# Doubling steps of a block inversion on 32x32 diagonal blocks held side by side, in a two-block model on one core

## The chip, the core and the metric

The kernel runs on one core of a Trainium2 chip. The metric is device time in microseconds (us) of one execution, the median of several runs. Engines are named as in the profile: PE is TensorE's matmul stream and PEld its weight loads, DVE is VectorE, ACT is ScalarE, POOL is GpSimd.

## The reference

The reference is a two-block model on 512 tokens of width 1024 (the first block has 256 context tokens more). The first block holds a bidirectional RWKV-7 mixer, an mLSTM mixer and two convolutional feed-forward parts; the second block runs twice a hybrid mixer whose main branch is a bidirectional gated delta rule. Both recurrent mixers are linear scans with a rank-one correction. The delta rule in chunks of 64 tokens reads:

```
lmat  = where(strict, einsum(k_beta, k) * decay, 0)
sol   = triangular_solve(eye + lmat, rhs, lower=True, unit_diagonal=True)
value, k_cum = sol[..., :dv], sol[..., dv:]
def step(state, inp):                 # over the chunks
    v_new = val_n - k_cum_n @ state
    o_n   = q_dec_n @ state + attn_n @ v_new
    state = state * decay_n + k_dec_n.T @ v_new
```

RWKV-7 is a plain scan in the reference; the kernel gives it the same chunked form. So for every chunk of 64, head and direction a unit triangular 64x64 matrix has to be inverted.

## The kernel before, in words

All large projections are fp32-accurate products made of three single-pass matmuls on split operands (`mmacc`, lines 344, 347 and 348: 128x128 weights, 512 or 256 columns). They make one long stream on TensorE. The recurrent work runs beside it as background generators, called strands: each yields after a small group of instructions with a planned cost and a planned delay, and `Kern.tick` steps those that are due between two groups of the stream. Two strands that share a `mate` are held so that they step together. The order in which each engine executes its instructions is fixed when the kernel is built.

There are four RWKV strands, one for each pair of heads. Pairs 0 and 1 start while the projections still run. When the projections are over, `K.finish` steps all four strands without a stream, together with the loads and matmuls of `ada_steps` (line 558). The first part of the output projection then runs beside pairs 2 and 3, and `K.drain` ends them. A pair makes 6 inversions, each of 8 matrices: 4 matrices side by side, for two heads one above the other (64 + 64 partitions), so a page is 128 partitions by 256 columns. In each of the two hybrid layers there are two strands with two heads each; a head makes one inversion of 16 matrices on a page of 128x512.

`Chunk.inverse` doubles the size of the inverted diagonal blocks: with W the inverse (transposed) for blocks of size s, one doubling is W := W - X·(L_s·W), where L_s is the matrix masked to the off-diagonal s-blocks (line 731, POOL) and X the transpose of W within blocks of 32 (line 742, DVE). It runs for s = 2, 4, 8, 16 and 32, and each doubling has two products of 64x64 matrices: line 739, whose result ACT copies to the page Z (line 743), and line 748, whose result DVE subtracts from W (line 749). Before the first doubling W is set up for s = 2 by elementwise operations (line 1153 for the RWKV pairs, lines in `gdn_head` for the delta rule). A matmul addresses the tile of the 128x128 array that lies at its operands' partitions: the products of the upper 64 and of the lower 64 partitions are on two different 64x64 tiles.

Of the kernel before, what the change touches and what calls it, by code (L numbers as in the profile page):

```python
# [10 lines left out]
AF = mybir.ActivationFunctionType  # L11
# [3 lines left out]
ADD, SUB, MUL, MAX = ALU.add, ALU.subtract, ALU.mult, ALU.max  # L15

P = 128
# [11 lines left out]
C64 = 64  # L29
# [3 lines left out]
GKH = 1  # L33
HOLD = 1500
INV = 1.25
NQ = 5
NR = 8

# [617 lines left out]
class Chunk:  # L656


    def __init__(self, K):
        nc = K.nc  # L660
        self.K = K

        def sel(ap, pattern, base, cm):
            nc.gpsimd.affine_select(out=ap, in_=ap, compare_op=ALU.is_ge, fill=0.0, base=base,
                                    pattern=pattern, channel_multiplier=cm)


        pm = [K.const([P, 2, 2, C64], name="pm") for _ in range(2)]
        nc.gpsimd.memset(pm[0], 1.0)
        for h in range(2):  # L670
            r = slice(64 * h, 64 * h + 64)
            for d in range(2):
                for x in range(2):
                    sel(pm[0][r, d, x], [[1 - 2 * d, C64]], -x, 2 * d - 1)
        nc.vector.tensor_copy(pm[1], pm[0])
        self.pm = pm

        self.zm = {}
        for s in (1, 2, 4, 8, 16, 32):
            m = K.const([P, 2, C64], name=f"zm{s}")  # L680
# [10 lines left out]
            self.zm[s] = m  # L691
# [12 lines left out]


        self.big = K.const([P, 2, C64], name="big64")
        nc.gpsimd.memset(self.big, 0.0)
        for h in range(2):
            r = slice(64 * h, 64 * h + 64)
            for d in range(2):  # L710
                nc.gpsimd.affine_select(out=self.big[r, d], in_=self.big[r, d], compare_op=ALU.is_ge, fill=1e30,
                                        base=0, pattern=[[1 - 2 * d, C64]], channel_multiplier=2 * d - 1)

    def pads(self, page):

        return [page(name="pad") for _ in range(2)]

    def inverse(self, Wp, Lp, Xp, pads):


        K = self.K
        nc = K.nc
        n = Wp.shape[1]
        nu, nb = n // C64, n // C64 // 2
        T4, U8 = "p (d c j) -> p d c j", "p (u j) -> p u j"
        Zp, Lm = [t[:, :n] for t in pads]
        W, X, Z, L = [t.rearrange(U8, u=nu) for t in (Wp, Xp, Zp, Lm)]
        hs = [slice(0, 64), slice(64, 128)]

        def masked(s):  # L730
            nc.gpsimd.tensor_tensor(Lm.rearrange(T4, d=2, c=nb), Lp.rearrange(T4, d=2, c=nb),  # L731
                                    self.zm[s][:, ::-1].unsqueeze(2).to_broadcast([P, 2, nb, C64]), MUL)

        masked(2)
        for s in (2, 4, 8, 16, 32):
            ps = K.ps()[:, :n]
            for u in range(nu):
                for r in hs:
                    nc.tensor.matmul(ps[r, u * 64:u * 64 + 64], L[r, u], W[r, u], start=True, stop=True)  # L739
            if s < 32:  # L740
                masked(2 * s)
            nc.vector.transpose(Xp, Wp)
            nc.scalar.activation(Zp, ps, AF.Copy)  # L743
            yield INV * n, 1000
            ps = K.ps()[:, :n]
            for u in range(nu):
                for r in hs:
                    nc.tensor.matmul(ps[r, u * 64:u * 64 + 64], X[r, u], Z[r, u], start=True, stop=True)  # L748
            nc.vector.tensor_tensor(Wp, Wp, ps, SUB)  # L749
            yield INV * n, 1000  # L750


def conv3(K, dst, ps, n, w0, w1, w2):
# [261 lines left out]
def rwkv_prep(K, CH, p, loc, rkv, lo, up, bon, seen, out, pads, SV, NV):  # L1015


    nc = K.nc
    T4 = "p (d c j) -> p d c j"
    n = C64 * NB  # L1020
    U = 2 * NB
    hs = [slice(0, 64), slice(64, 128)]
    two = len(K.env.ps) > 1
    s = loc[0][0]
# [29 lines left out]
    r, kk = kq[:, :2 * n], kq[:, 2 * n:4 * n]  # L1054
# [6 lines left out]
    for d in range(2):  # L1061
        t = cs[:, dsl(d)]
        t = t if d == 0 else t[:, ::-1]
# [52 lines left out]
    for t, m in ((kk, skew(0, S + 1, C64)), (r, skew(1, S - 1, C64))):  # L1116
        t = t.rearrange(T4, d=2, c=NB)
# [10 lines left out]
    Wp = K.p1(name="W")  # L1128
# [12 lines left out]
    for hh in ((0, 1),) if two else ((0,), (1,)):  # L1141
# [5 lines left out]
                                    MUL)  # L1147
        yield 500 * len(hh), 900
    W = Wp[:, :2 * n].rearrange("p (u j) -> p u j", u=U)
    KS = []  # L1150
    for h in range(2):
        t = RK[h].rearrange(u4, u=U, x=2)[:, :, 1]
        nc.vector.tensor_tensor(W[hs[h]], t[hs[h]], CH.i64[hs[h]].unsqueeze(1).to_broadcast([C64, U, C64]), ADD)
        nc.gpsimd.tensor_copy(t[hs[h]], KQ5[hs[h], 1])
        KS.append(t)
    ps = K.ps()
# [4 lines left out]
    Lp, Xp = b, kd  # L1161
    Lc = K.p1(name="L")
    nc.scalar.activation(Lc[:, :2 * n], ps[:, :2 * n], AF.Copy)
    yield 320, 300
    for hh in ((0, 1),) if two else ((0,), (1,)):
        pss = products(hh, C64, lambda q, u: k[q, 64 * u:64 * u + 64])
# [862 lines left out]
def gdn_head(K, CH, l, h, kqp, kq, v, zad, gcT, ngT, beT, bkT, eglT, gcd, egd, Ya, pads):  # L2029
    nc = K.nc  # L2030
    n = LT
    T4 = "p (d c j) -> p d c j"
# [11 lines left out]
    ps = K.ps()  # L2044
# [6 lines left out]
    ps = K.ps()  # L2051
# [33 lines left out]
    LTt = K.p2(name="LT").rearrange(T4, d=2, c=4)  # L2085
# [11 lines left out]
    Lp = K.p2(name="L")  # L2097
    nc.scalar.activation(Lp, pl, AF.Copy)
    yield 590, 600
    Wp = K.p2(name="W")  # L2100
    W = Wp.rearrange("p (u j) -> p u j", u=8)
    nc.vector.tensor_tensor(Wp.rearrange(T4, d=2, c=4), LTt, CH.zm[1].unsqueeze(2).to_broadcast([P, 2, 4, C64]), MUL)
    nc.vector.tensor_tensor(W, W, CH.i64.unsqueeze(1).to_broadcast([P, 8, C64]), ADD)
    K.free(LTt)
    Xp = K.p2(name="X")
    yield 0, 2000
# [6 lines left out]
    for st in range(8):  # L2113
# [40 lines left out]
        for d in range(2):  # L2154
            i, p = pos[d]
# [151 lines left out]
```

## Time and profile before

| quantity | value |
|---|---|
| median of 3 runs | 3422.88 us (3414.17 to 3428.34) |
| time of the profiled execution | 3418.44 us |
| its span in the trace | 3416.7 us |
| PE busy | 3151.7 us (92%), 25042 records |
| DVE busy | 2122.4 us (62%) |
| ACT busy | 1269.4 us (37%) |
| POOL busy | 614.0 us (18%) |

An fp32 matmul stands as two records of PE and two of PEld in the trace, a matmul of the split projections as one. The duration of a record is the time through the pipeline; records follow each other much faster than that, so the pace has to be read from the start of one record to the start of another.

### The profile page before, as it was taken

What the parts mean: (1) busy time and instruction counts of PE and PEld (TensorE: products, weight loads), DVE (VectorE), ACT (ScalarE), POOL (GpSimd) and SP (SyncE); (2) the same over time, 40 slices, a digit from 0 to 9 for tenths busy, and PEclk for the clock granted to TensorE, in tenths of its full rate; (3) what the DMA queues carried; (4) which work ended last, traced back from release to release, by engine and by line L of the source; (5) the groups of instructions that cost most, each with busy time, mean ns of one, the idle gap of its engine ahead of it and who ended that gap; (6) DMA issues with size and microseconds to landing.
All of it is one profiled execution on the core that took longest, in us unless ns stands there. A gap on an engine that the chain in (4) does not pass through costs nothing.

```text
span 3416.7 us, 61935 instructions
## 1 busy us (share of the span) xinstructions
PE 3151.7 (92%) x25042; PEld 2476.2 (72%) x25042; DVE 2122.4 (62%) x4318; ACT 1269.4 (37%) x2679; POOL 614.0 (18%) x762
## 2 busy tenths in 40 slices
PE   7999898888899999989888999988999899999988
PEld 4878676667688888868765888767667567766756
DVE  4444565645855555685666576677777666677665
ACT  4333343333432222364433332352433335233332
POOL 4111222211000000010010000005156000525500
PEclk8999998999999999999998999989999899999979
DMA  6432554431222222122222223232232343123332
GB/s 228 141 94 70 166 167 155 139 112 52 73 72 68 72 73 97 57 73 69 81 78 82 91 87 132 78 99 78 69 103 95 104 138 102 57 69 108 102 115 90
DMA packets 313570, 336.10 MB, mean 98 GB/s; under 512 B 26542, under 2 KB 259132, under 8 KB 313284
## 3 DMA queue, kind: packets, MB, share of 16 engines
q1 hardware_dynamic: 311172, 329.69, 30.0%
q8 instruction: 197, 3.23, 0.4%
q0 software_dynamic: 2112, 2.45, 0.3%
q14 instruction: 89, 0.73, 0.1%
HBM read 282.13 MB, written 49.94 MB: 97 GB/s over the span
## 4 chain that ended last, share of the span: by engine, by line
PE 61%; issue 18%; DVE 14%; ACT 3%; DMA 3%; POOL 0%; SPq 0%; DVEq 0%; POOLq 0%; ACTq 0%
PE mm L344 14%; PE mm L347 13%; PE mm L348 13%; DVE cfa L1794 3%; PE ps L739 2%; PE ps L748 2%; PE ps L1192 2%; DVE wl L81 2%; PE ps L1137 1%; PE ps L558 1%; PE ps L1719 1%; PE ps L2133 1%; DMA ld<-sp 1%; PE ps L2160 1%; PE ps L1701 1%
## 5 line engine op out<-in xcount | busy, mean ns | idle before, releaser
L344 PE MATMUL mm<-hl,wh 128*128 128x512 f32 (+1 forms) x3296 | 1249.6, 383 | 56.0 <-DVE qkv L1794 15.2
L347 PE MATMUL mm<-hl,wh 128*128 128x512 f32 (+1 forms) x3296 | 1225.8, 372 | 1.6 <-DVE hl L487 1.6
L348 PE MATMUL mm<-hl,wl 128*128 128x512 f32 (+1 forms) x3296 | 1218.5, 372 | 0.0
L344 PEld LDWEIGHTS mm<-hl,wh 128*128 128x128 f32 x3296 | 631.1, 192 | 192.8 <-issue 33.2
L348 PEld LDWEIGHTS mm<-hl,wl 128*128 128x128 f32 x3296 | 631.4, 192 | 114.6 <-issue 2.8
L347 PEld LDWEIGHTS mm<-hl,wh 128*128 128x128 f32 x3296 | 633.2, 192 | 106.3 <-DVE hl L487 3.4
L80 ACT ACTIVATE wh<-wr 128x512 fp32r<-128x512 f32 (+3 forms) x718 | 367.9, 561 | 704.2 <-PE mm L347 614.3
L81 DVE TENSOR_TENSOR wl<-wr,wh 128x512 fp32r<-128x512 f32 (+3 forms) x718 | 435.7, 640 | 230.1 <-ACT wh L80 205.2
L1372 DVE SCALAR_TENSOR_TENSOR cv<-mm,vecs,cv 128x441 f32<-128x441 f32 (+2 forms) x352 | 242.9, 692 | 94.3 <-ACT cv L1360 88.2
L1423 POOL MEMSET gwh<- 128x1024 f32 x3 | 2.9, 955 | 969.2 <-PE mm L347 969.2
L1794 DVE SCALAR_TENSOR_TENSOR cfa<-ld,vecs,cfa 128x497 f32<-128x497 f32 (+14 forms) x160 | 162.1, 1013 | 13.2 <-ACT cfa L1788 11.0
L1962 POOL TENSOR_SCALAR tap<-ld,vecs 128x498 f32<-128x498 f32 (+4 forms) x80 | 150.6, 1882 | 63.9 <-PE ps L2046 29.8
L1395 DVE TENSOR_TENSOR fy<-fy,mm 128x512 f32<-128x512 f32 x96 | 55.2, 577 | 126.3 <-PE mm L348 125.5
L1963 POOL TENSOR_TENSOR cfa<-cfa,tap 128x498 f32<-128x498 f32 (+4 forms) x80 | 112.1, 1401 | 5.3
L743 ACT ACTIVATE pad<-ps 128x256 f32<-128x256 f32 (+1 forms) x100 | 46.7, 468 | 155.5 <-PE ps L739 155.0
L2138 ACT ACTIVATE u<-ps,beT 64x128 f32<-64x128 f32 x128 | 46.2, 362 | 131.3 <-DVE u L2137 130.6
L1374 ACT ACTIVATE cv<-cv,vecs 128x256 f32<-128x256 f32 (+1 forms) x66 | 43.0, 652 | 132.1 <-DVE cv L1372 77.2
L749 DVE TENSOR_TENSOR cut<-cut,ps 128x256 f32<-128x256 f32 x120 | 49.3, 413 | 54.0 <-PE ps L748 53.2
L2137 DVE TENSOR_SCALAR u<-ps,kdT 64x128 f32<-64x128 f32 x128 | 44.5, 349 | 58.4 <-PE ps L2133 44.4
L1378 DVE TENSOR_TENSOR cv<-cv,mm 128x512 f32<-128x512 f32 x66 | 39.5, 599 | 65.5 <-ACT cv L1374 36.2
L425 PE MATMUL ps<-sq,one 128*128 128x512 f32 (+1 forms) x132 | 62.6, 609 | 15.8 <-ACT sq L395 13.7
L731 POOL TENSOR_TENSOR pad<-L,zm 128x512 f32<-128x512 f32 x40 | 54.4, 1360 | 113.4 <-PE ps L739 84.0
(479 smaller groups left out, 4418.9 us busy)
## 6 DMA issues: line engine op xcount, KB each, us to landing
ar<-in_ada_w_dram SPq DMA_DIRECT2D x96, 512.0 KB, 5.2
wr<-in_ffn_up_dram SPq DMA_DIRECT2D x44, 1024.0 KB, 5.0
wr<-in_w_in_dram SPq DMA_DIRECT2D x28, 1024.0 KB, 5.2
ld<-sp SPq DMA_DIRECT2D x84, 256.0 KB, 4.5
wr<-in_w_in_dram SPq DMA_DIRECT2D x32, 512.0 KB, 3.6
xsp<-x SPq DMA_DIRECT2D x48, 256.0 KB, 2.0
x<-xsp SPq DMA_DIRECT2D x48, 256.0 KB, 3.5
wr<-in_ffn_down_dram SPq DMA_DIRECT2D x20, 512.0 KB, 3.7
```

Source lines behind the costliest of these rows:

```text
L80: nc.scalar.activation(h[:, q:e], src, AF.Copy)
L81: nc.vector.tensor_tensor(l[:, q:e], src, h[:, q:e].bitcast(F32), SUB)
L344: mm = nc.tensor.matmul(ps[:m, :n], wh[:, i, :m], H[:, :n], start=first and i == 0, stop=False)
L347: nc.tensor.matmul(ps[:m, :n], wh[:, i, :m], L[:, :n], start=False, stop=False)
L348: nc.tensor.matmul(ps[:m, :n], wl[:, i, :m], H[:, :n], start=False, stop=last and i == nk - 1)
L739: nc.tensor.matmul(ps[r, u * 64:u * 64 + 64], L[r, u], W[r, u], start=True, stop=True)
L748: nc.tensor.matmul(ps[r, u * 64:u * 64 + 64], X[r, u], Z[r, u], start=True, stop=True)
L1192: nc.tensor.matmul(ps[hs[h], d], lhsT(d, h), rhs(d, h), start=first and i == 0 and d == 0, stop=last and i == len(parts) - 1, skip_group_c ...
L1372: nc.vector.scalar_tensor_tensor(t3[:, ro, co], a3[:, ri, ci], tap(ky, kx, ff), t3[:, ro, co], MUL, ADD)
L1794: nc.vector.scalar_tensor_tensor(dst[:, a:b], src[:, a + o:b + o], taps[j], dst[:, a:b], MUL, ADD)
L1962: nc.gpsimd.tensor_scalar(x[:, a:b], src[:, a + o:b + o], taps[j], None, MUL)
L1963: nc.gpsimd.tensor_tensor(g[:, a:b], g[:, a:b], x[:, a:b], ADD)
```

## The change: what it does

The first four doublings (s = 2, 4, 8, 16) touch only the 32x32 diagonal blocks, two for each 64x64 matrix. The change gathers these blocks: for each matrix a strip of 32 columns, so that partitions 0 to 31 hold the first diagonal block of the upper matrix, 32 to 63 its second, and so on. This halves the page (`compact`, in the second half of the two scratch pages that the inversion already had). The products of these doublings become four 32x32 matmuls for each former pair of 64x64 ones, on the four diagonal 32x32 tiles of the array (`quarters`); mask, transpose, copy and subtraction run over half the columns. The subtraction of s = 16 writes the four quarters back into a zeroed full page, in four instructions. The doubling s = 32 stays as it was. Setting up the compact W takes four instructions per page instead of two (RWKV) and five instead of two (delta rule), and the compact copy of L takes four more (POOL for RWKV, ACT for the delta rule). The yields of the compact doublings carry a smaller cost (`INQ` 0.8 against `INV` 1.25) and delay (900 against 1000).

```
+INQ = 0.8
+            if s < 32:
+                self.zq[s] = K.const([P, 2, 32], name="zq")
+                for q, o in self.quarters():
+                    nc.vector.tensor_copy(self.zq[s][q], m[q, :, o:o + 32])
...
+    def quarters(self):
+        return [(slice(32 * i, 32 * i + 32), 32 * (i % 2)) for i in range(4)]
+    def compact(self, pads, n):
+        return [t[:, n // 2:n].rearrange("p (u j) -> p u j", j=32) for t in pads]
...
     def inverse(self, Wp, Lp, Xp, pads):
+        Wc, Lc = self.compact(pads, n)
+        Xc, Zc, Mc = [t[:, :m].rearrange(U8, u=nu) for t in (Xp, Zp, Lm)]
+        def product(lhsT, rhs, blocks, w):
+            ps = K.ps()[:, :nu * w]
+            for u in range(nu):
+                for r in blocks:
+                    nc.tensor.matmul(ps[r, u * w:u * w + w], lhsT[r, u], rhs[r, u], start=True, stop=True)
...
-        for s in (2, 4, 8, 16, 32):
...
+        for s in (2, 4, 8, 16):
+            ps = product(Mc, Wc, qs, 32)
+            masked(2 * s)
+            nc.vector.transpose(Xp[:, :m], pads[0][:, m:n])
+            nc.scalar.activation(Zc, ps, AF.Copy)
+            yield INQ * n, 900
+            ps = product(Xc, Zc, qs, 32)
+            if s < 16:
+                nc.vector.tensor_tensor(Wc, Wc, ps, SUB)
+            else:
+                for q, o in self.quarters():
+                    nc.vector.tensor_tensor(W[q, :, o:o + 32], Wc[q], ps[q], SUB)
+            yield INQ * n, 900
+        ps = product(L, W, hs, 64)
...
 rwkv_prep:
+    nc.gpsimd.memset(Wp, 0.0)
-        nc.vector.tensor_tensor(W[hs[h]], t[hs[h]], CH.i64[hs[h]].unsqueeze(1).to_broadcast([C64, U, C64]), ADD)
+        for q, o in CH.quarters()[2 * h:2 * h + 2]:
+            nc.vector.tensor_tensor(Wc[q], t[q, :, o:o + 32], CH.i32[q].unsqueeze(1).to_broadcast([32, U, 32]), ADD)
+    for q, o in CH.quarters():
+        nc.gpsimd.tensor_copy(Lq[q], Lc[q, :2 * n].rearrange("p (u j) -> p u j", u=U)[:, :, o:o + 32])
 gdn_head:
+    for q, o in CH.quarters():
+        nc.scalar.activation(Lq[q], pl[q].rearrange("p (u j) -> p u j", u=8)[:, :, o:o + 32], AF.Copy)
+    nc.gpsimd.memset(Wp, 0.0)
```

TensorE's program before, in the stretch where the four strands run without the stream. L739 and L748 are the two products of a doubling, L1192 belongs to the scan, L1137 to the preparation; the names are destination, then moving and stationary operand, and the shape is that of the result:

```order
L748 MATMUL ps_6054<-cut_4223,bk_5460 64x64 x8
L748 MATMUL ps_6076<-pad_1643,bk_5152 64x64 x8
L739 MATMUL ps_5991<-cut_4237,cut_4232 64x64 x8
L739 MATMUL ps_6086<-cut_4229,cut_4224 64x64 x8
L1192 MATMUL ps_6115<-cut_1538,rk_5393 64x64
...
L1137 MATMUL ps_6179<-kq_5931,bk_5961 64x128
L1137 MATMUL ps_6180<-kq_5931,bk_5961 64x128
L1137 MATMUL ps_6179<-kq_5931,bk_5961 64x128
L748 MATMUL ps_6033<-cut_4231,bk_5597 64x64 x8
L748 MATMUL ps_6122<-cut_4223,bk_5460 64x64 x8
```

The same stretch of TensorE's program in the changed kernel, where L767 is the product of either size, L1238 the scan's line and L559 that of the `ada` matmuls:

```order
L767 MATMUL ps_5832<-pad_1325,pad_1326 32x32 x16
L1238 MATMUL ps_5870<-Pb_5830,cut_4637 64x64 x4
...
L1238 MATMUL ps_5877<-cut_4632,cut_4633 64x64
L767 MATMUL ps_5882<-pad_1325,bk_5140 32x32 x10
L767 MATMUL ps_5852<-cut_4645,cut_4639 64x64 x8
L559 MATMUL ps_4646<-ar_5863,csil_371 32x512 x4
L767 MATMUL ps_5882<-pad_1325,bk_5140 32x32 x6
L1238 MATMUL ps_5877<-cut_4632,cut_4636 64x64
```

A product has twice the matmuls now (16 for 8), and one of them is cut in two by 64x64 and 128x32 work of other strands.

DVE's program before, in the first hybrid layer, at the end of a head's inversion (L749 the subtraction, L742 the transpose, L81 the weight split of the stream, L1967 the convolution's sum):

```order
L749 TENSOR_TENSOR W_22559<-W_22559,ps_22825 128x512
L742 STREAM_TRANSPOSE X_22562<-W_22559 128x512
L81 TENSOR_TENSOR wl_23190<-wr_23187,wh_23189 128x512 x2
L749 TENSOR_TENSOR W_22809<-W_22809,ps_22918 128x512
L742 STREAM_TRANSPOSE X_22812<-W_22809 128x512
L749 TENSOR_TENSOR W_22559<-W_22559,ps_22936 128x512
```

The same place of DVE's program in the changed kernel (L780 the compact subtraction, L783 the one that writes the quarters back, L775 and L786 the transposes, L790 the last subtraction, L82 the split):

```order
L783 TENSOR_TENSOR W_24345<-pad_23995,ps_24862 32x8x32 x4
L786 STREAM_TRANSPOSE X_24376<-W_24345 128x512
L82 TENSOR_TENSOR wl_25205<-wr_25202,wh_25204 128x512 x2
L780 TENSOR_TENSOR pad_24226<-pad_24226,ps_24920 128x256
L775 STREAM_TRANSPOSE X_24720<-pad_24226 128x256
L2013 TENSOR_TENSOR cfa_25064<-cfa_25064,cfa_25065 128x512
L790 TENSOR_TENSOR W_24345<-W_24345,ps_25021 128x512
```

The subtraction of s = 16 is four instructions in a row here; those of the other compact doublings are half as wide.

## Rows read from the trace of the kernel before

**Rows 1.** The page: busy us, share and instructions of each engine.

```profile
PE 3151.7 (92%) x25042; PEld 2476.2 (72%) x25042; DVE 2122.4 (62%) x4318; ACT 1269.4 (37%) x2679; POOL 614.0 (18%) x762
```

**Rows 2.** Stages: length; busy of PE, PEld, DVE, ACT, POOL; clock, DMA, GB/s.

```profile
100.00:375.00 275.00, 274.75 (x3077) 223.77 (x3074) 124.32 (x276) 104.53 (x235) 50.69 (x89) 1.00 0.34 103
375.00:705.00 330.00, 283.43 (x5891) 216.41 (x5889) 208.62 (x526) 129.88 (x397) 94.71 (x172) 0.94 0.51 162
705.00:800.00 95.00, 87.72 (x980) 68.67 (x981) 33.64 (x85) 28.09 (x76) 9.96 (x17) 0.95 0.31 97
800.00:845.00 45.00, 38.06 (x685) 31.70 (x679) 25.94 (x67) 13.28 (x41) 11.98 (x16) 0.91 0.04 14
...
2345.00:2375.00 30.00, 22.47 (x245) 18.00 (x246) 25.45 (x28) 5.18 (x9) 23.99 (x16) 0.89 0.24 71
2375.00:2425.00 50.00, 50.00 (x566) 39.26 (x564) 29.66 (x54) 17.60 (x33) 8.67 (x7) 1.00 0.23 70
2425.00:2645.00 220.00, 208.04 (x1560) 152.18 (x1559) 167.19 (x290) 82.32 (x165) 117.34 (x81) 0.97 0.28 91
```

**Rows 3.** TensorE's timeline, hybrid: start, us, instruction, tile rows*columns, shape, count.

```profile
2379.93 0.39 PE L347 MATMUL mm<-hl,wh 128*128 128x512 f32 x1
2380.16 0.40 PE L348 MATMUL mm<-hl,wl 128*128 128x512 f32 x1
2380.49 2.08 PE L739 MATMUL ps<-W,pad 64*64 64x64 f32 x64
2382.50 0.50 PE L344 MATMUL mm<-hl,wh 128*128 128x512 f32 x1
2382.84 0.39 PE L347 MATMUL mm<-hl,wh 128*128 128x512 f32 x1
```

**Rows 4.** TensorE's timeline at two preparation steps of the pairs.

```profile
373.34 0.71 PE L1137 MATMUL ps<-cut,bk 64*64 64x64 f32 x32
...
539.79 0.27 PE L1137 MATMUL ps<-kq,bk 64*64 64x128 f32 x1
...
560.56 1.09 PE L1137 MATMUL ps<-kq,bk 64*64 64x128 f32 x16
```

**Rows 5.** TensorE's timeline in the stretch of strands alone.

```profile
568.34 0.40 PE L1192 MATMUL ps<-rk,cut 128*64 128x64 f32 x6
568.66 0.68 PE L739 MATMUL ps<-cut,cut 64*64 64x64 f32 x16
569.27 0.33 PE L1192 MATMUL ps<-rk,cut 128*64 128x64 f32 x2
569.53 0.45 PE L1192 MATMUL ps<-kq,cut 64*64 64x64 f32 x8
```

**Rows 6.** Groups by line and shape: busy us, mean ns, idle before.

```profile
L739 PE MATMUL ps<-W,pad 64*64 64x64 f32 x1280 | 48.9, 226 | 23.1 <-DVE W L749 23.1
L742 DVE STREAM_TRANSPOSE bk<-cut 128x256 f32<-128x256 f32 x120 | 53.0, 443 | 23.1 <-PE ps L1137 20.0
L742 DVE STREAM_TRANSPOSE X<-W 128x512 f32<-128x512 f32 x40 | 28.3, 706 | 1.1 <-PE ps L2095 0.4
L749 DVE TENSOR_TENSOR cut<-cut,ps 128x256 f32<-128x256 f32 x120 | 49.3, 413 | 54.0 <-PE ps L748 53.2
L749 DVE TENSOR_TENSOR W<-W,ps 128x512 f32<-128x512 f32 x40 | 26.9, 677 | 9.6 <-PE ps L748 9.3
L743 ACT ACTIVATE pad<-ps 128x512 f32<-128x512 f32 x40 | 23.9, 597 | 108.6 <-PE ps L739 108.5
L743 ACT ACTIVATE pad<-ps 128x256 f32<-128x256 f32 x60 | 22.9, 383 | 46.9 <-PE ps L739 46.5
L731 POOL TENSOR_TENSOR pad<-cut,zm 128x256 f32<-128x256 f32 x60 | 45.4, 756 | 141.9 <-PE ps L739 131.8 <-ACT cut L1163 8.4 <-issue 1.4
L1154 POOL COPY rk<-kq 64x256 f32<-64x256 f32 x48 | 22.8, 475 | 102.1 <-DVE cut L1153 101.4
L1153 DVE TENSOR_TENSOR cut<-rk,i 64x256 f32<-64x256 f32 x48 | 20.8, 433 | 1.0
```

More of the change, by code (lines that the diff above doesn't have):

```diff
@@ L676, in __init__ @@
         self.pm = pm
-        self.zm = {}
+        self.zm, self.zq = {}, {}
         for s in (1, 2, 4, 8, 16, 32):
-            m = K.const([P, 2, C64], name=f"zm{s}")
+            m = K.const([P, 2, C64], name=f"zm{s}") if s in (1, 32) else K.p1(shape=[P, 2, C64], name="zm")
             nb = C64 // (2 * s)
@@ L690, in __init__ @@
                     sel(v[r], [[2 * s, nb], [0, s]], o + s - 1, -1)
-            self.zm[s] = m
+            if s < 32:
+                self.zq[s] = K.const([P, 2, 32], name="zq")
+                for q, o in self.quarters():
+                    nc.vector.tensor_copy(self.zq[s][q], m[q, :, o:o + 32])
+            if s in (1, 32):
+                self.zm[s] = m
+            else:
+                K.free(m)
+        self.i32 = K.const([P, 32], name="i32")
+        for q, _ in self.quarters():
+            nc.vector.tensor_copy(self.i32[q], K.ident[q, q.start:q.start + 32])
         for h in range(2):
@@ L724, in inverse @@
         nu, nb = n // C64, n // C64 // 2
+        m = n // 2
         T4, U8 = "p (d c j) -> p d c j", "p (u j) -> p u j"
@@ L728, in inverse @@
         hs = [slice(0, 64), slice(64, 128)]
+        Wc, Lc = self.compact(pads, n)
+        Xc, Zc, Mc = [t[:, :m].rearrange(U8, u=nu) for t in (Xp, Zp, Lm)]
         def masked(s):
-            nc.gpsimd.tensor_tensor(Lm.rearrange(T4, d=2, c=nb), Lp.rearrange(T4, d=2, c=nb),
-                                    self.zm[s][:, ::-1].unsqueeze(2).to_broadcast([P, 2, nb, C64]), MUL)
-        masked(2)
-        for s in (2, 4, 8, 16, 32):
[L736 to L750, printed above, removed]
+            if s == 32:
+                nc.gpsimd.tensor_tensor(Lm.rearrange(T4, d=2, c=nb), Lp.rearrange(T4, d=2, c=nb),
+                                        self.zm[s][:, ::-1].unsqueeze(2).to_broadcast([P, 2, nb, C64]), MUL)
+            else:
+                v = "p (d c) j -> p d c j"
+                nc.gpsimd.tensor_tensor(Mc.rearrange(v, d=2), Lc.rearrange(v, d=2),
+                                        self.zq[s][:, ::-1].unsqueeze(2).to_broadcast([P, 2, nb, 32]), MUL)
@@ new lines, in product @@
+        def product(lhsT, rhs, blocks, w):
[3 more added lines that the diff above has]
+                    nc.tensor.matmul(ps[r, u * w:u * w + w], lhsT[r, u], rhs[r, u], start=True, stop=True)
+            return ps.rearrange(U8, u=nu)
+        masked(2)
+        qs = [q for q, _ in self.quarters()]
+        for s in (2, 4, 8, 16):
[7 more added lines that the diff above has]
+                nc.vector.tensor_tensor(Wc, Wc, ps, SUB)
+            else:
+                for q, o in self.quarters():
+                    nc.vector.tensor_tensor(W[q, :, o:o + 32], Wc[q], ps[q], SUB)
+            yield INQ * n, 900
@@ L753, in conv3 @@
+        ps = product(L, W, hs, 64)
+        nc.vector.transpose(Xp, Wp)
+        nc.scalar.activation(Z, ps, AF.Copy)
+        yield INV * n, 1000
+        ps = product(X, Z, hs, 64)
+        nc.vector.tensor_tensor(W, W, ps, SUB)
+        yield INV * n, 1000
 def conv3(K, dst, ps, n, w0, w1, w2):
@@ L1149, in rwkv_prep @@
     W = Wp[:, :2 * n].rearrange("p (u j) -> p u j", u=U)
+    nc.gpsimd.memset(Wp, 0.0)
+    Wc, Lq = CH.compact(pads, 2 * n)
     KS = []
@@ L2096, in gdn_head @@
     K.free(E)
-    Lp = K.p2(name="L")
+    Lp, Wp = K.p2(name="L"), K.p2(name="W")
     nc.scalar.activation(Lp, pl, AF.Copy)
+    Wc, Lq = CH.compact(pads, n)
+    for q, o in CH.quarters():
+        nc.scalar.activation(Lq[q], pl[q].rearrange("p (u j) -> p u j", u=8)[:, :, o:o + 32], AF.Copy)
     yield 590, 600
-    Wp = K.p2(name="W")
     W = Wp.rearrange("p (u j) -> p u j", u=8)
-    nc.vector.tensor_tensor(Wp.rearrange(T4, d=2, c=4), LTt, CH.zm[1].unsqueeze(2).to_broadcast([P, 2, 4, C64]), MUL)
-    nc.vector.tensor_tensor(W, W, CH.i64.unsqueeze(1).to_broadcast([P, 8, C64]), ADD)
+    nc.gpsimd.memset(Wp, 0.0)
+    for q, o in CH.quarters():
+        nc.vector.tensor_tensor(Wc[q].rearrange("p (d c) j -> p d c j", d=2), LTt[q, :, :, o:o + 32],
+                                CH.zq[1][q].unsqueeze(2).to_broadcast([32, 2, 4, 32]), MUL)
+    nc.vector.tensor_tensor(Wc, Wc, CH.i32.unsqueeze(1).to_broadcast([P, 8, 32]), ADD)
     K.free(LTt)
```

## The prediction

> **What bounds the kernel now.** The page comes first [rows 1]: TensorE is busy for 92% of the span, DVE for 62%, ACT for 37%, POOL for 18%. So a change in the strands is worth what it takes from TensorE's time, wherever TensorE has no gap, and the stages tell where that is [rows 2]. While the projections run beside pairs 0 and 1 (100 to 375 us) there is no gap at all. In the 330 us in which the four pairs run alone TensorE is busy for 283: the pairs wait for one another there, and TensorE's time still counts for most of it. In the drain after it (800 to 845) it is 38 of 45. In the hybrid layers the stretch at 2345 to 2375 is DVE's and POOL's (25 and 24 of 30, TensorE 22), the 50 us after it are TensorE's alone, and the next 220 nearly so (208). The second hybrid layer is built alike.
>
> **The products.** First the pace of the old ones. Two heads' products stand together as 64 records in 2.08 us [rows 3]; one lasts 0.226 [rows 6], so 63 steps from start to start take 1.86 us, 29.5 ns each. They alternate between two tiles, so one tile takes a record each 59 ns. That tiles work side by side is seen where four are in use [rows 4]: 32 records in 0.71 us, (0.71 - 0.22)/31 = 15.8 ns each, 63 for a tile. A tile's time depends on the columns: with 128 of them, on two tiles, where one lasts 0.27, it is (1.09 - 0.27)/15 = 54.7 ns a record [rows 4], 109 for a tile. From 109 at 128 columns to 59 at 64 is 0.78 ns a column; the line goes on to 34 ns at 32 columns, an estimate. Four tiles then give a record each 8.5 ns.
>
> A pair's product was 16 records, 0.47 us; it becomes 32 records, 32 x 8.5 = 0.27, so 0.20 less. A head's was 32 records, 0.94 us; it becomes 64, 0.54, so 0.40 less. There are 24 inversions of pairs and 8 of heads, and each has 8 such products: 192 x 0.20 + 64 x 0.40 = 64 us of TensorE less. The bounds: if a tile's time is proportional to the columns (29.5 ns), 74 us less. If a tile needs 59 ns whatever the width, four tiles give 14.8 ns for twice the records and nothing is saved. If no more than the pace seen on four tiles is to be had (15.8), 12 us are lost. I take the line, since between 128 and 64 columns it was measured and 32 is the next step.
>
> **The changes of tile shape.** They are what the change adds. One product between the 128x128 records of the stream costs more than its records [rows 3]: from the start of L348 before it (2380.16) to that of L347 behind it (2382.84) are 2.68 us. Two stream records at 0.23 us and 64 records at 29.5 ns are 2.35, so 0.33 us go to two changes of shape. Among the strands it is alike [rows 5]: from the start of the 64x64 records at 568.66 to the next shape at 569.27 are 0.61 us for 16 records (0.47): 0.14 over. The six records before took 0.32 us for 0.18, the two behind 0.26 for 0.06. So a change costs 0.14 to 0.20, also where both shapes are small; I take 0.15.
>
> How many there are can be counted in TensorE's program (the shape of each line's tiles is in the trace): 1211 before, 1517 in the changed kernel, 306 more, 46 us. They were few between strands, because nearly all small work had 64x64 tiles, and several products could follow one another; now 32x32 tiles stand between 64x64 ones. Lower bound of the price: the gap from the last old record (2382.50 - 0.15) to the stream, less the 59 ns that it needs anyway, 0.09 us, so 28 us; upper bound 0.20, 61 us.
>
> **By stages.** With the products of each stage counted in the program:
> - Beside the projections: 40 pair products, -8 us; 39 changes, +6. Net -2.
> - Pairs alone: 122 products, -24; 185 changes, +28. Net +3.
> - Output projection and drain: 30 products, -6; 25 changes, +4. Net -2.
> - Around the mLSTM: 6 changes, +1.
> - Each hybrid layer: 32 head products, -13; some 25 changes, +4. Net -9, twice -18. Some of it falls where TensorE waits anyway (2345 to 2375 and gaps later on), so I count 0.85 of it, -15.
>
> The sum is -15 to -16 us.
>
> **The other engines.** They come out even, for a reason that the groups show [rows 6]: an instruction has a fixed part. A transpose takes 443 ns at 256 columns and 706 at 512, 1.03 ns a column, so 311 at 128; a subtraction 413 and 677, so 281 at 128. A pair's inversion had five transposes, five subtractions and two set-up additions of 433 ns: 5.15 us. Now four transposes of 311 and one of 443, three subtractions of 281, four quarters of 281, one of 413 and four set-up additions of 300: 5.27 us. A head's: 8.3 before, 8.1 now. So DVE gains nothing. ACT saves 4 x 0.11 for a pair (by L743, 383 at 256 columns and 0.84 ns less a column); for a head it saves 4 x 0.21 and adds four copies of 0.38. POOL's mask goes from 0.76 to 0.45 us four times for a pair, but four copies of about 0.35 (475 ns at 256 columns) and a memset come in: +0.5 us, beside TensorE's preparation products. For a head POOL only gains, by its masks. None of the three binds there. What hides the added work is the planned delay of a strand (900 x 2.5 = 2250 ns of the planner's time behind each half doubling), in which TensorE works for the stream or for other strands. Without that cover a pair's chain is as long as before: -0.43 us by ACT, -0.40 by three subtractions, +0.71 by the quarters. The instructions added in the constants' set-up lie before the first stream record, beside loads. The smaller planned cost moves strands slightly ahead of the stream; the program shows the same work in each stage, with two scan products of the heads fewer left behind the matmuls of the convolution's branch, and I count nothing for it.
>
> The profiled execution took 3418.4 us. That is 4.5 below the median of the runs, 3422.9, and the measure is the median: 3423 - 16 = **3407 us**. A run of this kernel differs from another by 0.2 to 0.4%, so 0.5% (17 us) is about what can be told from no change; the forecast lies just inside.
>
> **The rivals.**
>
> *The narrow records are not quicker.* On a tile, 32 columns take the 59 ns of 64, or the engine can't issue more than four tiles at 15 ns a record. The products save nothing, the changes of shape stay: +6, +28, +4, +1 and 0.85 x 7.7 make +45, so 3468. It decides from a record of 40 ns on a tile, where 64 x (59 - 40)/(59 - 34) no longer pays for the changes. For it: no row has fewer than 64 columns on a tile of 64 or less, and the line has a fixed part (9 ns) already. Against it: the step from 128 to 64 shows next to no floor. The Trainium skill speaks for it: TensorEngine Tiling (Array Packing), section Performance Considerations, gives each matmul some 60 cycles of overhead, holds that one column takes as long as 60, and advises against taking a tiling factor from a dimension that is small already; by that the 32-column product would save almost nothing. The other page on it, TensorE: Matmul & The Clock Gate, Part 1, goes further: start to start never below about 25 ns, which would make 32 records 0.80 us and, over all products, about +106 us. The 15.8 ns between records on four tiles [rows 4] contradict that as a bound over tiles; for a single tile nothing here does. I give this rival 0.22.
>
> *The changes are cheap.* Where several strands are ready, a change of shape falls into time in which TensorE would have waited, and costs the bare 0.09: -5 beside the projections, -8 for the pairs alone, -4, +1 and 0.85 x -21 in the hybrids, together -33, so 3390. For it: TensorE waits 47 of 330 us in the pairs' stretch [rows 2]. Against it: beside the projections there is no gap to fall into. 0.18.
>
> *The quarters are late.* Four subtractions in a row are 4 x 0.41 = 1.65 us on a head's page for 0.68, and 1.12 for 0.41 on a pair's, and the pinned 64x64 product of s = 32 waits for the last of them, with the stream queued behind it on TensorE. If all of it shows, 8 x 0.97 + 24 x 0.71 = 25 us come back: 3432. For it: L749 kept TensorE waiting before as well. Against it: the planned delay is longer than the four. 0.12.
>
> The forecast itself has 0.48, with a range of its own from 3390 to 3420.
>
> **How the numbers follow.** The bound of 0.5% (3406) cuts the forecast's range in the middle, so half of its chance is faster and half the same. Faster: 0.24 + 0.18 = 0.42, less 0.01 = 0.41. The same: 0.24 and most of the late quarters, 0.34. Slower: the first rival and the rest, 0.25. The range reaches from a little below the cheap changes (3376) to near the first rival, 3462.
>
> **What would show it.** The 32x32 records: 32 of a pair's product from first start to last in about 0.27 us confirm the line, 0.47 the first rival. The start of the shape behind such a product, 0.14 to 0.20 us past what its records need. DVE's busy time within 1% of 2122 us. The pairs' stretch as long as before within 10 us, and each hybrid layer 5 to 10 us shorter. Wrong would make it: a drain of the array that is dearer for 32x32 tiles, TensorE's clock falling in new gaps, or strands that no longer meet, so that a product stands alone between two changes more often than counted.

## The result, and the profile after

| quantity | before | after |
|---|---|---|
| median of 6 runs each, on the same chip | 3424.18 us | 3463.01 us (3451.08 to 3473.32) |
| ratio | | 1.0118, 95% interval 1.0091 to 1.0145 |
| profiled execution, its span | 3416.7 us [rows 1 give its engines] | 3469.7 us |

The change makes the kernel slower by 1.2%. The forecast was 3407, and 3463 lies 1 us past the upper end of the range, though near the time that the first rival gave. The profiled execution of the changed kernel lies 8 us above its median, and that of the kernel before 6 us below its own, so the spans differ by 53 us where the medians differ by 39: some 14 us of the differences below are those of single executions.

The page of the changed kernel, busy time of each engine, answers to [rows 1]:

```profile
PE 3192.1 (92%) x30162; PEld 2471.6 (71%) x30162; DVE 2112.5 (61%) x4510; ACT 1266.9 (37%) x2713; POOL 612.4 (18%) x890
```

DVE, ACT and POOL are where they were, within 1%. PE is busy for 40 us more, although its new products are shorter (from first to last start 0.26 us at full clock, where the old ones took 0.46). Where that is, the windows of both kernels show when they are cut at the same records of the stream. Columns as in [rows 2]; the third from the end is the mean granted clock. Before: the pairs alone; the first stretch behind the drain; the two hybrid layers.

```profile
372.40:695.20 322.80, 277.25 (x5831) 212.82 (x5831) 200.08 (x508) 125.61 (x385) 90.11 (x164) 0.94 0.50 160
832.70:956.10 123.40, 103.97 (x527) 78.33 (x526) 86.84 (x205) 55.85 (x122) 7.22 (x11) 0.92 0.22 74
2200.50:2797.20 596.70, 544.64 (x3759) 402.82 (x3758) 412.86 (x771) 225.37 (x442) 182.17 (x131) 0.93 0.30 97
2797.20:3416.70 619.50, 552.99 (x3825) 413.50 (x3823) 407.57 (x759) 222.30 (x445) 184.57 (x134) 0.92 0.29 92
```

The changed kernel: ahead of it the stretch beside the projections, then the same four.

```profile
100.00:375.00 275.00, 273.33 (x3698) 219.09 (x3699) 127.15 (x306) 100.75 (x234) 52.57 (x118) 1.00 0.34 104
374.30:743.10 368.80, 309.15 (x7673) 219.72 (x7672) 197.11 (x578) 120.72 (x380) 92.77 (x236) 0.81 0.42 134
882.20:1016.10 133.90, 113.90 (x608) 85.16 (x607) 89.27 (x213) 56.94 (x126) 8.17 (x11) 0.87 0.20 69
2269.30:2861.10 591.80, 539.29 (x4784) 394.62 (x4783) 406.43 (x795) 226.97 (x458) 178.08 (x135) 0.93 0.31 98
2861.10:3469.70 608.60, 548.63 (x4849) 406.96 (x4847) 400.84 (x783) 224.86 (x461) 180.86 (x138) 0.91 0.30 94
```

| stage | predicted | measured (spans) |
|---|---|---|
| to the end of the projections (372.4, 374.3) | -2 | +2 |
| pairs alone (322.8, 368.8) | +3 | +46 |
| output projection and drain (137.5, 139.1) | -2 | +2 |
| from the drain to the hybrids (1367.8, 1387.1) | +1 | +19 |
| both hybrid layers (1216.2, 1200.4) | -15 | -16 |

The hybrid layers did what was forecast. The loss is in the pairs' stretch, and there one column has moved that the forecast held constant: the mean granted clock, 0.94 before and 0.81 now. TensorE has two levels, so 0.81 means that 2 x (1 - 0.81) = 38% of the stretch, 140 us, ran at 1.2 GHz instead of 2.4; before it was 39 us.

What the lower level does is seen on TensorE's timeline of the changed kernel; the first two rows are at full clock, the next four some 10 us later, at the lower level, and the last at full clock again.

```profile
424.15 0.45 PE L767 MATMUL ps<-cut,bk 32*32 32x32 f32 x32
424.53 0.45 PE L1238 MATMUL ps<-cut,cut 128*64 128x64 f32 x8
...
433.79 0.65 PE L767 MATMUL ps<-cut,bk 32*32 32x32 f32 x32
434.24 0.63 PE L767 MATMUL ps<-cut,cut 32*32 32x32 f32 x32
434.79 0.69 PE L1238 MATMUL ps<-Pb,cut 64*64 64x64 f32 x8
...
436.20 1.94 PE L559 MATMUL ps<-ar,csil 128*32 128x512 f32 x8
...
604.89 1.06 PE L559 MATMUL ps<-ar,csil 128*32 128x512 f32 x8
```

The same product of 32 records lasts 0.45 us and then 0.65; eight `ada` records last 1.94, and 1.06 later on where the clock is full again. The windows around these rows, with TensorE busy for all of their length, show the two levels as 1.00 and 0.50:

```profile
424.00:425.60 1.60, 1.60 (x68) 1.40 (x64) 1.54 (x4) 0.66 (x2) 0.40 (x1) 1.00 0.75 246
...
432.40:435.80 3.40, 3.40 (x112) 3.10 (x112) 0.68 (x3) 1.05 (x4) 1.88 (x6) 0.50 0.12 34
```

### The profile page after: what moved, and what is told of

The parts are those of the page before. It is cut to its first block, busy times and chain, and to the rows that moved or that the text cites. A ratio compares the mean times of both kernels' runs of the same rounds, so it can differ in the third digit from the quotient of the medians.

```text
span 3469.7 us, 72527 instructions
## 1 busy us (share of the span) xinstructions
PE 3192.1 (92%) x30162; PEld 2471.6 (71%) x30162; DVE 2112.5 (61%) x4510; ACT 1266.9 (37%) x2713; POOL 612.4 (18%) x890
## 4 chain that ended last, share of the span: by engine, by line
PE 75%; DVE 14%; ACT 4%; issue 3%; DMA 3%; POOL 1%; SPq 0%; DVEq 0%; POOLq 0%; ACTq 0%
PE mm L345 19%; PE mm L348 17%; PE mm L349 17%; PE ps L767 4%; DVE cfa L1840 3%; PE ps L1238 3%; PE ps L1178 2%; PE ps L559 2%; DVE wl L82 1%; PE ps L1765 1%; PE ps L2184 1%; PE ps L426 1%; PE ps L2196 1%; PE ps L2211 1%; PE ps L1747 1%
## 5 line engine op out<-in xcount | busy, mean ns | idle before, releaser
L345 PE MATMUL mm<-hl,wh 128*128 128x512 f32 (+1 forms) x3296 | 1252.2, 384 | 45.4 <-DVE qkv L1840 13.8
L349 PE MATMUL mm<-hl,wl 128*128 128x512 f32 (+1 forms) x3296 | 1220.5, 372 | 0.0
L345 PEld LDWEIGHTS mm<-hl,wh 128*128 128x128 f32 x3296 | 631.4, 192 | 182.6 <-issue 34.4
L349 PEld LDWEIGHTS mm<-hl,wl 128*128 128x128 f32 x3296 | 631.6, 192 | 116.2 <-issue 4.0
L81 ACT ACTIVATE wh<-wr 128x512 fp32r<-128x512 f32 (+3 forms) x718 | 367.8, 561 | 659.6 <-PE mm L348 567.9
L82 DVE TENSOR_TENSOR wl<-wr,wh 128x512 fp32r<-128x512 f32 (+3 forms) x718 | 432.9, 637 | 215.2 <-ACT wh L81 198.6
L1840 DVE SCALAR_TENSOR_TENSOR cfa<-ld,vecs,cfa 128x497 f32<-128x497 f32 (+14 forms) x160 | 152.5, 953 | 10.1 <-ACT cfa L1834 7.7
L559 PE MATMUL ps<-ar,csil 128*32 128x512 f32 x384 | 76.7, 790 | 7.1 <-DMA ar<-in_ada_w_dram 5.4
L767 PE MATMUL ps<-pad,pad 32*32 32x32 f32 x3584 | 53.0, 199 | 28.0 <-DVE pad L780 27.8
L767 PEld LDWEIGHTS ps<-pad,pad 32*32 32x32 f32 x3584 | 42.1, 110 | 49.8 <-issue 27.8
L2188 DVE TENSOR_SCALAR u<-ps,kdT 64x128 f32<-64x128 f32 x128 | 43.8, 348 | 55.1 <-PE ps L2184 46.5
```

Source lines behind the costliest of these rows:

```text
L81: nc.scalar.activation(h[:, q:e], src, AF.Copy)
L82: nc.vector.tensor_tensor(l[:, q:e], src, h[:, q:e].bitcast(F32), SUB)
L345: mm = nc.tensor.matmul(ps[:m, :n], wh[:, i, :m], H[:, :n], start=first and i == 0, stop=False)
L349: nc.tensor.matmul(ps[:m, :n], wl[:, i, :m], H[:, :n], start=False, stop=last and i == nk - 1)
L559: m = nc.tensor.matmul(ps[32 * c:32 * c + 32, :], self.csil[:, k, :], raw[c // 2][:, 512 * (c % 2):512 * (c % 2) + 512], start=k == 0, sto ...
L767: nc.tensor.matmul(ps[r, u * w:u * w + w], lhsT[r, u], rhs[r, u], start=True, stop=True)
```

## The experiments

These rows leave two theories, and a third beside them. **A, the clock**: the narrow products give TensorE's array less to do, its clock is granted at the lower level more often, and that costs more than the products save. **B, the changes of shape**: between 32x32 and other tiles they cost far more than the 0.15 us that were counted, and the clock only follows the waiting. **C, the planner**: the smaller numbers in the yields pull the strands apart. Two kernels take the two halves of the narrow product apart, 32x32 tiles with the old 64 columns, and 64x64 tiles with 32 columns.

### Tiles alone: 32x32 tiles, 64 columns

The second product is cut in the same way; the doubling s = 32 stays as it was.

```
-                for r in hs:
-                    nc.tensor.matmul(ps[r, u * 64:u * 64 + 64], L[r, u], W[r, u], start=True, stop=True)
+                for r, o in quarters(s):
+                    nc.tensor.matmul(ps[r, u * 64:u * 64 + 64], L[r, u, o], W[r, u], start=True, stop=True)
...
```

> The kernel before, with the products of the first four doublings cut into 32x32 tiles but left at 64 columns; all other engines as before. TensorE's program has 1467 changes of tile shape (1211 before, 1517 after the whole change), 176 of the 256 new ones in the stretch of the pairs alone. The records should need what they needed (32 records in about 0.47 us). Theory A, the shorter products leave TensorE with too little to do and its clock is granted at 1.2 GHz more often: nothing is shortened here, so time at 1.2 GHz in the pairs' stretch stays near the 37 us of before, and only the changes cost, 256 x 0.15 = 38 us, 3462 in all, pairs' stretch +26. Theory B, the changes of shape themselves cost far more than 0.15 among the strands (the 46 us lost there and the 24 saved are 70 us for 185 changes, 0.38 each): pairs' stretch +67, about 3500 in all, at an unchanged clock. Theory C, the smaller planned costs pull the strands apart: planned costs are as before here, so no loss beyond the 38 us.

Measured: 3511.5 us, 1.0246 of before (1.0230 to 1.0261). The pairs' stretch, and a product in it with the next shape:

```profile
375.40:750.30 374.90, 318.18 (x7745) 229.15 (x7743) 199.34 (x507) 128.30 (x385) 88.83 (x163) 0.88 0.43 138
```

```profile
599.07 0.65 PE L753 MATMUL ps<-cut,bk 32*32 32x64 f32 x32
599.65 1.06 PE L558 MATMUL ps<-ar,csil 128*32 128x512 f32 x8
```

The records need what was expected, (0.65 - 0.22)/31 = 14 ns each. The stretch is 52 us longer, between A's 26 and B's 67, and the clock fell here too, to 0.88: 90 us at the lower level. So neither number of mine held. With the price of the lower level from the next runs (0.43 us lost per us) the 51 us more of it are 22 us. The changes of shape in this stretch, counted in the traces by the tile of each record, rose from 272 to 427, so by 155 and not the 176 that I had expected: 155 x 0.15 = 23. Together that is 45 of the 52. B's 0.38 for a change is not needed. Why the clock fell here, though no column was taken away, is not shown: the smaller tiles or the 11 us more in which TensorE waits (374.90 - 318.18 against 322.80 - 277.25) may be the reason. The two hybrid layers lost 24 us as well, for 27 more changes:

```profile
2266.10:2877.40 611.30, 549.04 (x4783) 403.83 (x4782) 413.25 (x771) 224.07 (x442) 184.12 (x131) 0.92 0.31 95
2877.40:3506.80 629.40, 561.25 (x4849) 418.40 (x4847) 409.40 (x759) 223.37 (x446) 183.92 (x134) 0.91 0.30 91
```

The changes are 4 us of that, and 28 us more at the lower level (by the clock records of the traces, 204 against 176) are 12; the other 8 stay open.

### Columns alone: 64x64 tiles, 32 columns

The copy and the subtraction read the 32 columns twice, so that ACT's and DVE's pages stay as wide as before. The inverse is not computed here.

```
+            w = 64 if s == 32 else 32
...
-                    nc.tensor.matmul(ps[r, u * 64:u * 64 + 64], L[r, u], W[r, u], start=True, stop=True)
+                    nc.tensor.matmul(ps[r, u * w:u * w + w], L[r, u], W[r, u, :w], start=True, stop=True)
...
+            nc.scalar.activation(Zp if s == 32 else twice(Zp), ps if s == 32 else wide(ps), AF.Copy)
```

> The kernel before, with the products of the first four doublings on their 64x64 tiles but with 32 columns instead of 64; the copy and the subtraction read the 32 columns twice, so that ACT and DVE do as much as before (the inverse is not computed in this kernel). No change of tile shape is added (1200 against 1211). A pair's product should take 16 records at 17 ns, 0.27 us, as short as in the changed kernel. Theory A (clock): time at 1.2 GHz in the pairs' stretch rises from 37 us toward the 143 of the changed kernel, at least to 70, and the 24 us that the products save there are lost again: the stretch within 10 us of before; in all 3395 to 3420. Theory B (changes of shape): no changes, so the whole saving is seen: pairs' stretch -24, in all about 3423 - 8 - 24 - 6 - 22 = 3363, clock as before. Theory C (planned costs): the same as B.

Measured: 3482.5 us, 1.0163 of before (1.0143 to 1.0182). The pairs' stretch, a product on the timeline, and the subtraction and copy that read twice:

```profile
371.50:736.80 365.30, 317.76 (x5825) 245.88 (x5823) 198.85 (x505) 125.43 (x383) 90.48 (x164) 0.80 0.45 143
```

```profile
520.95 0.66 PE L755 MATMUL ps<-pad,bk 64*64 64x32 f32 x16
```

```profile
L756 DVE TENSOR_TENSOR cut<-cut,ps 128x256 f32<-128x256 f32 x120 | 49.7, 415 | 68.5 <-PE ps L755 67.9
L750 ACT ACTIVATE pad<-ps 128x256 f32<-128x256 f32 x60 | 22.7, 381 | 53.3 <-PE ps L746 52.5 <-ACT cut L1175 0.3 <-PE ps L1144 0.2
```

Two things are to be seen. The stretch is 42 us longer and its clock 0.80, as in the changed kernel, though there is no 32x32 tile, no new change of shape, and copy and subtraction last as long as before (381 and 415 ns against the 383 and 413 of [rows 6]). And the product is hardly shorter: 0.66 us for 16 records against 0.68 [rows 5], that is 29 ns a record, not the 17 that I expected. So TensorE does not wait more because of the product; it does fewer columns in the same time, and the clock goes. Of the expectations, A had the lower level right (at least 70 us; 146 by the clock of the row) and the time wrong: it let the products' saving pay for the clock, a stretch within 10 us of before and 3395 to 3420 in all, and the saving did not come. B and C had neither. The hybrid layers are 7 us longer here as well (1223.4 against 1216.2):

```profile
2260.50:2863.20 602.70, 547.79 (x3759) 405.13 (x3758) 415.55 (x771) 224.46 (x442) 183.30 (x131) 0.93 0.31 96
2863.20:3483.90 620.70, 555.77 (x3825) 415.86 (x3823) 405.73 (x759) 223.36 (x446) 185.20 (x134) 0.92 0.30 92
```

### The columns given back, and not read

The same kernel with 64 columns again in each matmul; copy and subtraction still read 32 of them, twice (so no inverse here either).

```
-                    nc.tensor.matmul(ps[r, u * w:u * w + w], L[r, u], W[r, u, :w], start=True, stop=True)
+                    nc.tensor.matmul(ps[r, u * 64:u * 64 + 64], L[r, u], W[r, u], start=True, stop=True)
...
```

> The kernel of the run with 32 columns, given its 64 columns back: every product of the first four doublings streams 64 columns on the 64x64 tiles again, but copy and subtraction still read only 32 of them, twice (the inverse is not computed here either). Against the run with 32 columns the only difference is that each matmul streams 32 further columns whose result nobody reads; the records needed 27 to 29 ns each with either width there. Theory A (fewer columns let TensorE's clock be granted at 1.2 GHz): the useless columns bring the clock back; time at 1.2 GHz in the pairs' stretch about 40 us instead of 147, the stretch about 323 us instead of 365, in all about 3425. Rival D (the loss of the 32-column run came from its operand data or from the doubled reads of ACT and DVE): it stays near 3480, stretch near 365.

Measured: 3425.9 us, 1.0001 of before (0.9988 to 1.0014), as A forecast. The pairs' stretch, and the subtraction and the copy, to be held against the same two rows of the run with 32 columns:

```profile
371.80:696.90 325.10, 281.27 (x5833) 214.94 (x5831) 200.16 (x508) 125.44 (x385) 90.04 (x164) 0.93 0.50 159
```

```profile
L755 DVE TENSOR_TENSOR cut<-cut,ps 128x256 f32<-128x256 f32 x120 | 49.3, 413 | 54.2 <-PE ps L754 53.3
L749 ACT ACTIVATE pad<-ps 128x256 f32<-128x256 f32 x60 | 22.8, 382 | 45.7 <-PE ps L745 45.2
```

32 useless columns per record take the stretch from 365.3 back to 325.1 us. Rival D falls: both kernels compute the same values, and copy and subtraction last as long. Nor are there new gaps with 32 columns: PE is idle for 47.5 us of its stretch in 46 gaps, the longest of 3.1 us, and with 64 columns for 43.8 us in 48 gaps, the longest of 4.5. The other 36 us are busy time. This is the pair of runs that settles the theory, and it gives the price: the narrow products saved (0.68 - 0.66) x 122 = 2 us, the stretch lost 40, so 43 us (the medians of first to last start at full clock, 420 to 432 against 463 ns, give 4 to 5 us saved, and a price some 0.02 higher) belong to 2 x (0.20 x 365.3 - 0.07 x 325.1) = 101 us more at the lower level: 0.43 us for each. The Trainium skill (TensorE: Matmul & The Clock Gate, section Terms) puts the penalty at the throttled time multiplied by one less the share of clock pulses that pass, which is one half here; the measured 0.43 is close to it and goes into the sums here. The hybrid layers of the run with 32 columns bear the price out: they have 18 us more at the lower level than the kernel before (194 against 176, by the clock records), which makes 8 us by it, and they are 7 us longer.

### Useless work in the changed kernel

```
...
+            if w == 32 and nu == 4:
+                nc.tensor.matmul(bank[:, P:4 * P], self.fill, self.fill.unsqueeze(1).to_broadcast([P, 3, P]),
+                                 start=True, stop=True)
```

> The changed kernel with one useless 128x128 matmul of 384 columns behind each narrow product of the pairs (126 of them in the stretch of the pairs alone; its result is not read). By its own time, 0.16 us and one to two changes of shape of 0.15, each costs TensorE 0.31 to 0.46 us, 39 to 58 us in that stretch. Theory A (clock): time at 1.2 GHz in the stretch falls from 143 us to below 80; at 0.4 us lost for each of those, at least 25 us come back, so the stretch is 369 + 39 to 58 - 25 to 40 = 370 to 400 us. Rival B (the loss has nothing to do with the clock): the stretch grows by the whole of the useless work, 408 to 427 us.

Measured: 3486.1 us, 1.0178 of before (1.0156 to 1.0200). The pairs' stretch, and one of the added matmuls on the timeline:

```profile
379.70:751.10 371.40, 329.12 (x7728) 225.61 (x7727) 193.77 (x567) 119.91 (x377) 92.87 (x236) 0.87 0.41 131
```

```profile
563.94 0.45 PE L770 MATMUL ps<-pad,pad 32*32 32x32 f32 x32 [1.68 <-DVE pad L786]
564.32 0.44 PE L772 MATMUL ps<-fill 128*128 128x384 f32 x1
564.69 0.45 PE L1244 MATMUL ps<-cut,rk 128*64 128x64 f32 x8
```

One of them takes 0.37 us from its start to the next shape. The trace has 120 of them in this stretch, not the 126 expected, so 44 us, and PE is busy for 20 us more. The stretch is longer by 2.6, inside A's 370 to 400 and outside rival B's 408 to 427. The granted clock rose from 0.81 to 0.87, from 140 us at the lower level to 97, worth 19 us at 0.43; that is less than A forecast (below 80 us). Another 18 us fell into gaps (PE had 60 us of them in 368.8, and has 42 now), which the expectation had not counted; 5 us stay open. Even with those 18 us in gaps rival B's stretch would be 395 us long. Where the clock is full anyway the filler only costs: the projections end at 379.7 us instead of 374.3, and the whole kernel is slower than the changed one (1.0178 of before against 1.0118).

### The old planned costs in the changed kernel

```
-INQ = 0.8
+INQ = 1.25
-            yield INQ * n, 900
+            yield INQ * n, 1000
```

> The changed kernel with the planned cost and delay of the old doublings (1.25 and 1000 instead of 0.8 and 900). Theory C (the smaller numbers pull the strands apart): the loss goes, about 3407, pairs' stretch near 325 us. Theories A and B: within 12 us of the changed kernel's 3463, pairs' stretch 355 to 380 us, time at 1.2 GHz in it above 110.

Measured: 3462.4 us, 1.0101 of before (1.0086 to 1.0116), against the 3463.0 of the changed kernel; the pairs' stretch took 371 us at the same clock:

```profile
370.60:741.60 371.00, 314.87 (x7751) 221.93 (x7749) 199.56 (x583) 121.44 (x386) 94.08 (x238) 0.82 0.44 140
```

This is what A and B had forecast; C falls for the pairs' stretch. From the drain to the hybrid layers this kernel took 1377.4 us, 10 more than before where the changed kernel took 19 more.

### The change in the hybrid layers alone

The pairs keep the old inversion and its set-up; only `gdn_head` calls the compact one. To make room for the masks of both, the identity is added in four quarters in a head, three DVE instructions more.

```
-    yield from CH.inverse(Wp[:, :2 * n], Lc[:, :2 * n], Xp, pads)
+    yield from CH.inverse_full(Wp[:, :2 * n], Lc[:, :2 * n], Xp, pads)
```

> The change in the two hybrid layers alone; the RWKV pairs keep the 64x64 products of before and their set-up. All theories: up to 2200 us as before, since the loss was read there (46 us in the pairs' stretch, 14 behind it); the first hybrid layer 5 us shorter and the second 11, as in the changed kernel's trace; about 3407. If the hybrids' gain hung on the time at which they are reached, within 5 us of before.

Measured: 3423.2 us, 0.9988 of before (0.9977 to 0.9999). The two hybrid layers:

```profile
2209.30:2809.50 600.20, 543.84 (x4783) 398.36 (x4782) 412.01 (x807) 226.85 (x458) 179.58 (x135) 0.91 0.31 97
2809.50:3422.80 613.30, 551.71 (x4849) 408.53 (x4847) 406.60 (x795) 224.88 (x461) 181.65 (x138) 0.91 0.30 93
```

The loss of the pairs is gone, but so is most of the gain: the first layer is 3.5 us longer than before, the second 6.2 shorter. The 3407 forecast was missed; with 4 us less than before, the other outcome named there came, within 5 us. With the old planned costs (the edit of the run before):

> The 32x32 products in the hybrid layers alone (the pairs as before), with the old planned cost and delay (1.25 and 1000). With the smaller numbers this version took 0.9988 of before, 4 us; in the changed kernel the old numbers made the hybrid layers shorter by 1 and 3 us. Up to 2200 us as before. If the hybrids' gain is that of the products, 3410 to 3420, a ratio of 0.996 to 0.999; if it is given back to the clock there as well, 0.999 to 1.002.

Measured: 3418.0 us, 0.9977 of before (0.9966 to 0.9989), inside the forecast and the fastest of all versions, though a gain of 8 us only.

```profile
2206.70:2800.20 593.50, 539.25 (x4783) 395.29 (x4782) 415.33 (x807) 227.40 (x458) 176.75 (x135) 0.92 0.31 98
2800.20:3410.30 610.10, 543.70 (x4849) 403.02 (x4847) 410.44 (x795) 224.77 (x461) 174.95 (x138) 0.92 0.30 94
```

The layers are 3.2 and 9.4 us shorter. The versions with narrow heads (the one with useless work aside) thus gain 3 us, 13, 16 (the changed kernel) and 17 (the changed kernel with the old planned costs, 1199.4) in the hybrids. The clock moves along with it: by the clock records of the traces these layers ran 176 us at the lower level before, and 214, 198, 194 and 180 in these four. At 0.43 that took back 16, 9, 8 and 2 us, so that without it the gains would be 19, 22, 24 and 19 us. This is an estimate, from one execution of each; why the same products lower the clock more in one order of the strands than in another is not shown.

## Why the prediction was wrong

**The pace of the products: right.** 64 records of a head's product between stream records, to be held against [rows 3]:

```profile
2397.76 0.40 PE L349 MATMUL mm<-hl,wl 128*128 128x512 f32 x1
2398.09 0.75 PE L767 MATMUL ps<-pad,pad 32*32 32x32 f32 x64
2398.77 0.50 PE L345 MATMUL mm<-hl,wh 128*128 128x512 f32 x1
```

From the start of L349 to that of L345 are 1.01 us, 0.23 for the stream record, (0.75 - 0.19) = 0.56 for 63 steps, 8.9 ns each, so 0.22 for two changes of shape. A pair's 32 records took (0.45 - 0.20) = 0.25 to 0.26 us; 0.27 was forecast, and 0.54 for a head. The reason that I gave, a line in the columns, was only half right: on a 64x64 tile, 32 columns still took 29 ns a record, 58 for the tile; on a 32x32 tile 64 columns took 14 ns a record, 56 for the tile. Only a smaller tile together with fewer columns is quicker. The line passed through the right point because width and tile were halved together.

**The price of a change of shape: right, rather on its lower side; their number was too high.** From the product at 424.15 to the next shape are 0.38 us, 0.13 past its records; in the stream it is 0.11 for each; in the run with the tiles alone 0.58 - 0.43 = 0.15 (from 599.07 to 599.65). Counted in the traces, the changes in the pairs' stretch rose from 272 to 425, by 153 where the sum has 185, and in the whole kernel by 278 where it has 306. At 0.13 to 0.15 the 153 are 20 to 23 us, not 28.

**The stages: the step that failed.** "Pairs alone: 122 products, -24; 185 changes, +28. Net +3" was summed at the clock of before. The first term holds and the second is 5 to 8 us too high, but a third was missing: the time at the lower clock, which the products had kept short. With it, -24 + 20 to 23 + 0.43 x (140 - 39) = +39 to +42, and +46 was measured; some 5 us stay open. I did name TensorE's clock as what would make the forecast wrong, but as something that falls in new gaps, and gave it neither a price nor a chance. The changed kernel does wait 14 us more in this stretch (60 against 46), but the run with columns alone, at 0.80, shows that no new gap is needed. Its pair with the columns given back was run on 64x64 tiles. For the 32x32 tiles the step from 64 columns (0.88) to 32 (0.81) points the same way, and so do the useless matmuls (0.87); how much of the fall there is due to columns, tile and gaps each is not shown.

From the drain to the hybrids 19 us were lost where 1 was forecast. Ten of them lie in the first stretch behind the drain, at a clock of 0.87 instead of 0.92, that is 35 us at the lower level instead of 20, 6 us by the same price; the pairs' last work runs into it. The rest lies in later stretches, and no run took it apart; it is gone where the pairs keep their old products (1370 us for the stage with narrow heads alone). Since the same stage lost 10 us with the old planned costs, part of the 19 may be that of a single execution.

**The hybrid layers: right, in part by luck**, -16 against -15. The forecast took 18 us for products and changes and a deduction for TensorE's waits; the runs with heads alone gained 3 and 13 us, and the estimate above makes it some 19 to 24 us for products and changes, less what the clock took back, a term that the forecast did not have.

**The other engines: right.** The groups of the changed kernel, as in [rows 6], and below them the 64x64 products of s = 32:

```profile
L775 DVE STREAM_TRANSPOSE bk<-cut 128x128 f32<-128x128 f32 x48 | 14.9, 310 | 6.0 <-PE ps L1178 4.8
L780 DVE TENSOR_TENSOR cut<-cut,ps 128x128 f32<-128x128 f32 x36 | 10.2, 284 | 26.6 <-PE ps L767 26.3
L783 DVE TENSOR_TENSOR cut<-cut,ps 32x128 f32<-32x128 f32 x48 | 13.5, 282 | 9.7 <-PE ps L767 8.9
L1197 DVE TENSOR_TENSOR cut<-rk,i 32x128 f32<-32x128 f32 x48 | 13.9, 290 | 1.0
L776 ACT ACTIVATE pad<-ps 128x128 f32<-128x128 f32 x48 | 13.2, 275 | 31.1 <-PE ps L767 30.4
L760 POOL TENSOR_TENSOR cut<-cut,zq 128x128 f32<-128x128 f32 x48 | 22.4, 467 | 82.7 <-PE ps L767 80.2 <-DMA cut<-rkv 1.7
L767 PE MATMUL ps<-cut,cut 64*64 64x64 f32 x192 | 11.5, 256 | 4.9 <-DVE cut L783 4.3 <-issue 0.6
L767 PE MATMUL ps<-W,pad 64*64 64x64 f32 x256 | 11.1, 232 | 2.8 <-DVE W L783 1.8 <-POOL cfa L2009 1.0
```

310, 284, 282, 290, 275 and 467 ns stand against the 311, 281, 281, 300, 273 and 450 that the sum used.

**The rivals.** *The narrow records are not quicker* gave 3468, 5 us from what came, and is refuted all the same: the records are as quick as forecast, so its number came near by luck. Its claim is true of the 64x64 tile, where half the columns saved 0.02 of 0.68 us. There this agrees with the Trainium skill (TensorEngine Tiling (Array Packing), section Performance Considerations), which lets one column take as long as 60; on the 32x32 tile 8.4 ns a record at 32 columns against 14 at 64 contradict it. The bound of 25 ns from start to start, which the prediction names as well, does not hold over four tiles: it is 8.4 there. *The changes are cheap* did not come. *The quarters are late* is refuted by the last two rows above: the 64x64 product waited 4.3 us for L783 among the pairs and 1.8 in the heads (0.2 more in other groups), of 25 feared.

## What to carry to other kernels

Where a stretch has small matmuls alone, count what a change takes from TensorE's array, and read the granted clock of that stretch before summing times: with 32 columns the products of the pairs' stretch saved 2 us, and the stretch lost 40. In this kernel narrower work did less harm where a dense stream stands around it (the hybrid layers, some 18 us more at the lower level) than where small matmuls stand alone (the pairs' stretch, 101 more). Taking an edit apart into its two sizes, columns and tile, and giving one of them back as useless work, told the clock from the changes of shape and gave its price; a run with the old planned costs ruled out the order as the cause of that stretch's loss.

## What the runs showed of the hardware

- On two 64x64 tiles a record of 32 columns starts every 29 ns, against 30 to 31 for one of 64; on four 32x32 tiles every 8.4 ns at 32 columns and every 14 at 64.
- The same stretch with the same number of matmuls and the same ACT and DVE work was granted 0.93 of the full clock with 64 columns in the products and 0.80 with 32, with about the same gaps (43.8 and 47.5 us).
- One us at 1.2 GHz cost 0.43 us of a stretch in which TensorE is busy for 86 to 87% of the time.
- A change of tile shape between matmuls cost TensorE 0.11 us in the dense stream and 0.13 to 0.15 us among small matmuls.
